# Encoder layer on one core: key and query projections of the second mixer by seven half-size products each

## The chip, the core and the metric

The kernel runs on one core of one Trainium2 chip. The metric is the device time of one execution in microseconds (us); lower is better. TensorE is called PE here, VectorE DVE, ScalarE ACT, GpSimd POOL, and SyncE, which issues DMAs, SP.

## The reference

One layer of a bidirectional encoder, width 1024, sequence 512, batch 1, everything in float32. Cut to what matters:

```python
mod = silu(c) @ w_mod + b_mod                     # nine vectors of 1024: shifts, scales, gates
h = modulate(rmsnorm(x, norm_ffn1), sh1, sc1)
x = x + 0.5 * g1 * swiglu(h, w_ffn1_in, w_ffn1_out)          # first FFN
h = modulate(rmsnorm(x, norm_mix), sh2, sc2)
qa, ka, va, qb, kb, vb, ga, gb = split(h @ w_in)  # 512 128 128 512 512 512 1024 1024 columns
ya = window_gqa_sink(rope(rmsnorm(qa)), rope(rmsnorm(ka)), va, sink) @ w_branch_a
qb = rope(rmsnorm(qb)); kb = rope(rmsnorm(kb))    # per head of 64, 8 heads of each
ob = diff_attention(qb, kb, vb, lam)              # softmax(q1 k1) - lam softmax(q2 k2), times vb
yb = (rmsnorm(ob, subln_b) * (1 - lam_init)) @ w_branch_b
x = x + g2 * ((sigmoid(ga) * ya + sigmoid(gb) * yb) @ w_out)
h = modulate(rmsnorm(x, norm_ffn2), sh3, sc3)
x = x + 0.5 * g3 * swiglu(h, w_ffn2_in, w_ffn2_out)          # second FFN
```

The change concerns `kb` and `qb`, each a product of h (512 x 1024) and a slice of `w_in` (1024 x 512).

## The kernel before, in words

**Products.** Every float32 product is made as three products of shorter floats: an operand is split into a high part (a CAST on ACT) and a low part (original less high, a TENSOR_TENSOR on DVE), both by `split_from` (L190), and high x high, high x low and low x high are added in PSUM. Names: `high` and `low` are the parts of a weight tile, `raw` or `u` its loaded float32, `b` a tile of activations or of their parts, `acc`, `sc`, `op` and `tp` are PSUM banks, `f` and `sm` scratch.

**The FFNs** run their large products as Strassen-Winograd units: a product of 2 x 2 blocks is made of seven products of half size for eight. A `Unit` goes through its items s1, a11, a12, s2, s4, s3, a22; four of these names are sums of blocks of weights (s1 = a21 + a22, s2 = s1 - a11, s3 = a11 - a21, s4 = a12 - s2), made by loading one block with SP and adding another with an accumulating DMA from POOL's queue into the same tile. `MAKE` says how many items ahead a weight is split. The other operand comes from `h_sum` (n1, n2, t3, t4: sums of blocks of h). `two` (L458 to L460) issues a product's instructions, with weights held and 256 columns of h moving.

**The boundary** ends the first FFN, computes the norm, and writes h by `hidden`, in tiles of 128x256: ACT writes the high part (L355), DVE the low part (L363). Three gates are begun beside it, nine PE instructions a tile.

**main** then issues, in this order, the projections of values, keys and queries of the second mixer (`project`, L1202 to L1204: 96 instructions each, h held, 512 columns of weights moving), the remaining gates (`gates`, weights by `load_main`: ACT writes high and the negative, L1132 and L1134, and POOL adds the original by an accumulating DMA, L1135), and the projections of the first mixer (`project_pairs`, L1222 to L1224, h held, 256 columns moving). Of keys and queries each block of 128 rows gets a norm and a rotation: ACT squares (L1255), DVE reduces (L1256), POOL takes the power -1/2 (L1261), DVE multiplies and adds (L1271 to L1274); keys are also multiplied by their norm (L1317), while the query's norm enters later, in the softmax, and `freq` holds its negative (L1340). Then PE transposes (L1281) and the result is split. Scores (L187) follow.

**Order.** Instructions of an engine run in the order in which the program issues them. The pieces of attention are not called where they stand: `Line` keeps an estimate of PE's and DVE's time and calls a piece when it is due (`line.at`, `line.helped`). `beside` puts a column of the modulation product (`mod_col`, a DVE instruction over 128x1024 with its own load of w_mod, L283) after every so many steps of a projection: `LATER` is that number there, `EARLY`, `NEXT` and `SIDE` say how many columns go elsewhere. Tiles come from rings: `raw`, `u` (`u4` in the code), `f` and `b` (`b8`, and `high`, `low`) each have a fixed number of buffers, so a load waits until the last reader of an older tile is done.

Of the kernel before, what the change touches and what calls it, by code (L numbers as in the profile page):

```python
# [11 lines left out]
F32 = mybir.dt.float32  # L12
# [3 lines left out]
ALU = mybir.AluOpType  # L16
AX = mybir.AxisListType

P = 128
# [92 lines left out]

EARLY, NEXT, SIDE, LATER = 3, 3, 0.27, 4
BESIDE_MIX = (1, 2, 2, 2, 2, 1)
# [20 lines left out]
def layer(ctx: ExitStack, tc: tile.TileContext, a: dict):  # L135
# [212 lines left out]
    def hidden(rb, c, sc, sh, hi, lo, r=FULL[0], value=None):  # L348

        t = f2()[:, r]  # L350
        s = modv[sh][:, c : c + 1]
        if value is not None:
            rb = rb[:, r]
        V.scalar_tensor_tensor(t, x[c][:, r], modv[sc][:, c : c + 1], rb, ALU.mult, ALU.mult)
        S.activation(hi[:, r], t, AF.Identity, bias=s)  # L355
        yield
        if value is not None:
            if r.stop - r.start == T:
                t3 = t.rearrange("p (t q) -> p t q", t=2)
            else:  # L360
                t3 = t.unsqueeze(1)
            S.activation(value, t3, AF.Identity, bias=s)
        V.scalar_tensor_tensor(lo[:, r], t, s, f(hi[:, r]), ALU.add, ALU.subtract)  # L363
        yield
# [7 lines left out]
    def boundary(parts, g, norm, sc, sh, hh, hl, into, ahead, at):  # L372
# [16 lines left out]
        def h_steps(rs, r):  # L389

            before = None
# [60 lines left out]
    def two(po, w, k, x, first, last, js=range(2)):  # L452

        (wh, wl), (xh, xl) = w, x
        for j in js:
# [4 lines left out]
            PE.matmul(out, wl[:, s], xh, start=False, stop=last and j == 1, skip_group_check=True)  # L460

    class Unit:

# [13 lines left out]

        in_order, by_columns, asides = (), (), {}
        spare, roomy, apart, more = ("s1",), (), (), {"s1": ("s2", "a11"), "s2": ("s4", "a12"), "a11": ("s3", "a21")}
# [16 lines left out]
        def prepare(self, q):  # L496
# [5 lines left out]
            if q in self.apart:  # L502
                both = b8().rearrange("p a b -> p (a b)")
                hi, lo = both[:, 0:n], both[:, 1024 : 1024 + n]
            else:
                hi, lo = high_low(n, self.asides.get(q, ASIDE), (self, q))
            t = self.at[q]
# [8 lines left out]
        def multiply(self, q, ks=None):  # L516
# [6 lines left out]
            for js in ((0,), (1,)) if q in self.by_columns else (range(2),):  # L523
                for k in ks:
                    x = self.operand(OPERAND[q], k)
                    two(po, self.ready[q], k, x, new and k == 0, k == self.depth - 1, js)
            if self.depth - 1 in ks:
# [20 lines left out]

    def run_items(items):


# [20 lines left out]
        for n, (u, q, ks, also) in enumerate(items):  # L572
            begin(n)
            if also is not None:
                also()
            u.multiply(q, ks)
            if ks is None or u.depth - 1 in ks:
                u.after(q)
            begin(n)
# [21 lines left out]

    def h_sum(t):

        p, q = SUMS[t]
        hq[t] = hq[q if t in ("t3", "t4") else p]

        h_op[t] = [u4() for _ in range(2)] if t == "n1" else b8()
        for i in range(2):
            r = slice(i * T, (i + 1) * T)
            sub(hq[t][:, r], hq[p][:, r], hq[q][:, r], t in NEGATED)  # L610
        for i in range(2):
            v = hq[t][:, i * T : (i + 1) * T].rearrange("p (k q) -> p k q", k=2)
            o = h_op[t][i] if t == "n1" else h_op[t][:, 2 * i : 2 * i + 2, :]
            split_from(o[:, :, T1], o[:, :, T2], v)
# [340 lines left out]
    def item1(u, q, ks=None):  # L955
        items1.append((u, q, ks, side1))

    credit, asked = [0.0], []

    room = b8(F32).rearrange("p a b -> p (a b)")  # L960
    room = [room[:, i * 1024 : (i + 1) * 1024] for i in range(2)]

    def column(columns):
# [5 lines left out]
        if asked and (len(asked) > COLUMNS[columns is rest] or not columns):  # L969
            mod_col(*asked.pop(0), in_order=columns is not later)  # L970

    def side1(n=SIDE):

        while small_loads and len(rest) < 20:
            nc.sync.dma_start(*small_loads.pop())
# [181 lines left out]
    def first_gates(r):  # L1157
# [3 lines left out]
        for k in range(NC):  # L1161
# [7 lines left out]
            yield  # L1169

    vb_w = boundary(
        last1, G1, n2, SC2, SH2, hh, hl, first_gates,
# [17 lines left out]

    def project(srcs, n, then):

        per = 1024 // n
        out = [bank("acc" if t < 3 else "sc") for t in range(NT)]
        for u in range(NC // per):
            wh, wl = srcs.pop(0) if isinstance(srcs, list) else load_halves(srcs[u])
            for t in range(NT):
# [52 lines left out]

    def head_stats(raw, nh, rs, scale8):

        sq = f2()
        n = nh * HD
        S.activation(sq[:, 0:n], raw, AF.Square)  # L1255
        V.tensor_reduce(rs, sq[:, 0:n].rearrange("p (h d) -> p h d", d=HD), axis=AX.X, op=ALU.add)  # L1256
        if scale8:
            V.tensor_scalar(rs, rs, HD * EPS, None, ALU.add)
        else:
            V.tensor_scalar(rs, rs, 1.0 / HD, EPS, ALU.mult, ALU.add)  # L1260
        G.tensor_tensor(rs, rs, half[:, 0:nh], ALU.pow)  # L1261
        return sq

    def rope(raw, nh, tabs, t, z):
        C, R = tabs
        n = nh * HD
        y = f2()
        r3 = raw.rearrange("p (h d) -> p h d", d=HD)
        y3 = y[:, 0:n].rearrange("p (h d) -> p h d", d=HD)
        z3 = z[:, 0:n].rearrange("p (h d) -> p h d", d=HD)  # L1270
        V.tensor_tensor(y3, r3, C[:, t, :].unsqueeze(1).broadcast_to([P, nh, HD]), ALU.mult)  # L1271
        for o, i in ((slice(0, NF), slice(NF, HD)), (slice(NF, HD), slice(0, NF))):
            V.tensor_tensor(z3[:, :, o], r3[:, :, i], R[:, t, o].unsqueeze(1).broadcast_to([P, nh, NF]), ALU.mult)
        V.tensor_tensor(y[:, 0:n], y[:, 0:n], z[:, 0:n], ALU.add)  # L1274
        return y

    def turned(srcs, tag="tp"):
# [10 lines left out]

    def turn_heads(y, nt, t, hi, lo, then=None):
        ht = slice(t * P, (t + 1) * P)  # L1290
        v = turned(cut(y, nt)).rearrange("p (j q) -> p j q", j=nt)
        with tc.high_priority():
            split_from(hi[:, 0:nt, ht], lo[:, 0:nt, ht], v)
        turns["t"] = t + 1
        if then is not None:
            line.at(line.free["tp"] + SLACK, then, SCORES)

    def raws(ps, n=T):
# [5 lines left out]

    def queries(ps, tabs, rq, hi, lo, then):
        for t, raw in enumerate(raws(ps)):
            z = head_stats(raw, 8, rq[:, t, :], True)
            y = rope(raw, 8, tabs, t, z)
            due = line.helped(2.6, 2.5) + SLACK
            line.at(due, lambda y=y, t=t: turn_heads(y, 4, t, hi, lo, then if t == 1 else None), ("tp",))  # L1310

    def keys(raw, nh, tabs, t, hi, lo):
        rs = small(nh)
        z = head_stats(raw, nh, rs, False)
        y = rope(raw, nh, tabs, t, z)
        y3 = y[:, 0 : nh * HD].rearrange("p (h d) -> p h d", d=HD)
        V.tensor_tensor(y3, y3, rs.unsqueeze(2).broadcast_to([P, nh, HD]), ALU.mult)  # L1317
        due = line.helped(0.4 * nh, 2.5) + SLACK
        line.at(due, lambda: turn_heads(y, nh * HD // P, t, hi, lo), ("tp",))
# [6 lines left out]
    done, turns = {"a": 0, "b": 0}, {"a": 0, "b": 0, "o": 0, "w": (0, 0), "q": 0, "t": 0}  # L1326

    def keys_b(ps):
        for t, raw in enumerate(raws(ps)):
            keys(raw, 8, table["kb"], t, kb_h, kb_l)  # L1330

# [4 lines left out]

    def queries_b(ps):
        queries(ps, table["qb"], rqb, qb_h, qb_l, lambda: diff_scores(0, 0))
        for t in range(NT):
            V.tensor_scalar(nrqb[:, t, :], rqb[:, t, :], -1.0, None, ALU.mult)  # L1340

    head_b = {}

    def diff_scores(h, b0):
# [45 lines left out]
        if nxt[0] < 4:  # L1390
            line.at(
                start + 2 * PERIOD_B, lambda: diff_scores(*nxt), SCORES + (lambda: unit - turns["b"] < DEPTH_B - 1 and turns["t"] == NT,)
            )
# [663 lines left out]
def lay_out(i):  # L2057
# [61 lines left out]
```

## Time and profile before

| | |
|---|---|
| median of 3 runs | 1034.4 us (1034.29 to 1034.94) |
| the profiled execution, its own time | 1034.51 us |
| its span in the profile | 1032.7 us |
| busy: PE, DVE, ACT, POOL | 1027.6, 787.4, 582.1, 161.8 us |
| PE instructions (matmul) | 7346 |
| DMA | 220.39 MB, mean 213 GB/s |

The span runs from the first to the last instruction that the profile holds; the execution's time has 1.8 us more around it. The rows of the profile give an engine, the line of the kernel that issued the instruction (L190 is a helper that many call), output and inputs with buffer numbers left out, shapes as partitions x elements, and a count. A row of the timeline begins with its start in us from the start of the span and its duration; in brackets stands how long the engine was idle before it and what ended that. PE overlaps its instructions, so a PE row's duration (0.39) is longer than the step from one start to the next (0.23), and the steps are what counts.

### The profile page before, as it was taken

The page shows a single profiled execution, that of the slowest core. Times are in us where ns is not written, and L with a number is a line of the kernel's source. Part 1 is how long each engine was busy: PE and PEld are TensorE (multiplying, and loading weights), DVE is VectorE, ACT ScalarE, POOL GpSimd, SP SyncE. Part 2 cuts the span into 40 slices and gives each one's busy share as a digit, 9 for nine tenths or more (in the row PEclk, how much of TensorE's full clock was granted, in tenths as well). Part 3 has the DMA queues.
Part 4 walks back from the last instruction along what each step waited for, and adds up shares of the span by engine and source line. Part 5 has one row for each costly group of instructions (what it writes and reads, how often), then busy time and mean ns, then how long its engine had stood idle before and what let it go on. Part 6 is the DMA issues. An engine that isn't in the chain of part 4 may idle for free.

```text
span 1032.7 us, 18848 instructions
## 1 busy us (share of the span) xinstructions
PE 1027.6 (100%) x7346; PEld 949.0 (92%) x7346; DVE 787.4 (76%) x1457; ACT 582.1 (56%) x1013; POOL 161.8 (16%) x189
## 2 busy tenths in 40 slices
PE   9999999999999999999999999999999999999998
PEld 7889899899998998899888888989999999999998
DVE  7886667567787679859772588976898777877877
ACT  6755335244454443668785856525877556655553
POOL 1101110110100100543323101001112112212210
PEclk9999999999999999999999999999999999999999
DMA  9977887967875459796737944974498998989974
GB/s 363 371 207 202 239 241 219 251 153 243 218 188 158 144 213 410 237 281 135 181 79 185 259 136 151 367 250 103 93 239 195 238 236 209 222 228 215 207 158 113
DMA packets 70233, 220.39 MB, mean 213 GB/s; under 512 B 8448, under 2 KB 13184, under 8 KB 70144
## 3 DMA queue, kind: packets, MB, share of 16 engines
q1 hardware_dynamic: 47808, 146.52, 39.2%
q0 software_dynamic: 19200, 68.17, 35.9%
q10 hardware_dynamic: 3136, 4.51, 1.2%
q8 instruction: 57, 0.93, 0.4%
q14 instruction: 32, 0.26, 0.1%
HBM read 208.94 MB, written 10.23 MB: 212 GB/s over the span
## 4 chain that ended last, share of the span: by engine, by line
PE 96%; DVE 2%; ACT 2%; issue 0%; POOL 0%; DVEq 0%; ACTq 0%
PE acc L460 7%; PE acc L459 7%; PE acc L458 7%; PE sc L460 6%; PE sc L458 6%; PE sc L459 6%; PE sc L174 5%; PE sc L176 5%; PE sc L175 5%; PE acc L174 5%; PE acc L176 5%; PE acc L175 5%; PE tp L1281 2%; PE acc L709 2%; PE acc L1203 2%; PE acc L1202 2%
## 5 line engine op out<-in xcount | busy, mean ns | idle before, releaser
L190 ACT CAST high<-raw 128x1024 fp32r<-128x1024 f32 (+2 forms) x176 | 158.4, 914 | 149.4 <-PE sc L175 40.8
L190 DVE TENSOR_TENSOR low<-raw,high 128x1024 fp32r<-128x1024 f32 (+2 forms) x176 | 183.5, 1052 | 40.4 <-ACT high L190 38.8
L459 PE MATMUL acc<-b,high 128*128 128x256 f32 x508 | 140.5, 277 | 0.1
L458 PE MATMUL acc<-b,high 128*128 128x256 f32 x508 | 140.6, 277 | 0.0
L460 PE MATMUL acc<-b,low 128*128 128x256 f32 x508 | 140.5, 277 | 0.0
L460 PE MATMUL sc<-b,low 128*128 128x256 f32 x500 | 138.0, 276 | 0.0
L458 PE MATMUL sc<-b,high 128*128 128x256 f32 x500 | 138.0, 276 | 0.0
L459 PE MATMUL sc<-b,high 128*128 128x256 f32 x500 | 138.0, 276 | 0.0
L190 ACT CAST high<-u 128x1024 fp32r<-128x1024 f32 (+1 forms) x73 | 75.4, 1034 | 52.3 <-PE sc L175 20.0
L190 DVE TENSOR_TENSOR low<-u,high 128x1024 fp32r<-128x1024 f32 (+1 forms) x73 | 87.7, 1201 | 21.5 <-ACT high L190 20.0
L174 PE MATMUL sc<-b,high 128*128 128x512 f32 (+1 forms) x272 | 97.4, 358 | 0.0
L175 PE MATMUL sc<-b,high 128*128 128x512 f32 (+1 forms) x272 | 97.0, 357 | 0.0
L176 PE MATMUL sc<-b,low 128*128 128x512 f32 (+1 forms) x272 | 97.0, 357 | 0.0
L459 PEld LDWEIGHTS acc<-b,high 128*128 128x128 f32 x508 | 95.4, 188 | 0.5 <-DVE b L1903 0.3
L458 PEld LDWEIGHTS acc<-b,high 128*128 128x128 f32 x508 | 95.4, 188 | 0.2
L460 PEld LDWEIGHTS acc<-b,low 128*128 128x128 f32 x508 | 95.4, 188 | 0.1
L460 PEld LDWEIGHTS sc<-b,low 128*128 128x128 f32 x500 | 93.9, 188 | 0.0
L458 PEld LDWEIGHTS sc<-b,high 128*128 128x128 f32 x500 | 93.9, 188 | 0.0
L459 PEld LDWEIGHTS sc<-b,high 128*128 128x128 f32 x500 | 93.9, 188 | 0.0
L174 PE MATMUL acc<-b,high 128*128 128x512 f32 (+1 forms) x240 | 89.2, 372 | 0.0
L176 PE MATMUL acc<-b,low 128*128 128x512 f32 (+1 forms) x240 | 86.6, 361 | 0.0
L175 PE MATMUL acc<-b,high 128*128 128x512 f32 (+1 forms) x240 | 86.5, 360 | 0.0
(400 smaller groups left out, 2717.9 us busy)
## 6 DMA issues: line engine op xcount, KB each, us to landing
u<-w_mod SPq DMA_DIRECT2D x38, 512.0 KB, 8.0
b<-w_mod SPq DMA_DIRECT2D x32, 512.0 KB, 5.5
raw<-w2i SPq DMA_DIRECT2D x31, 512.0 KB, 5.6
u<-w2i POOLq DMA_DIRECT2D x31, 512.0 KB, 6.8
raw<-w1u SPq DMA_DIRECT2D x24, 512.0 KB, 6.5
u<-w1u POOLq DMA_DIRECT2D x24, 512.0 KB, 7.1
raw<-w1o SPq DMA_DIRECT2D x24, 384.0 KB, 4.8
raw<-w_gate SPq DMA_DIRECT2D x16, 512.0 KB, 5.4
```

Of the source, the lines that this page charges most:

```text
L174: PE.matmul(out, wh, xh, start=first, stop=False)
L175: PE.matmul(out, wh, xl, start=False, stop=False)
L176: PE.matmul(out, wl, xh, start=False, stop=last)
L190: last = S.copy(hi, src), V.tensor_tensor(lo, src, f(hi), ALU.subtract)
L458: PE.matmul(out, wh[:, s], xh, start=first and j == 0, stop=False, skip_group_check=True)
L459: PE.matmul(out, wh[:, s], xl, start=False, stop=False, skip_group_check=True)
L460: PE.matmul(out, wl[:, s], xh, start=False, stop=last and j == 1, skip_group_check=True)
L709: PE.matmul(out1[i][:, r], w[:, i * P : (i + 1) * P], h[:, r], start=first and r.start == 0, stop=last and r.stop == T, skip_group_check=True,
L1202: PE.matmul(out[t][:, 0:n], hh[k][:, ht], wh[:, o : o + n], start=k == 0, stop=False)
L1203: PE.matmul(out[t][:, 0:n], hh[k][:, ht], wl[:, o : o + n], start=False, stop=False)
L1281: PE.transpose(tp[:, j * P : (j + 1) * P], src, ident)
```

## The change

Keys and queries are each made by a `Unit`: seven products of half size, with h held and 256 columns of weights moving (`two_turned`), 7 x 24 = 168 instructions where 96 of 512 columns stood. The weights are laid out by quarters. The first sum of weights (s1) of the key's unit is loaded and added ahead of the boundary. `hidden` writes h also as float32 (an ACT instruction for each tile, L356), from which the four sums of h are made at the start of `main`. Results come by quarters of 256 rows and 256 columns (two blocks of rows, four heads), in the unit's order, and the norm and rotation are made by `two_blocks`, which the first mixer had already: L1507 ACT square, L1508 reduce, L1513 POOL's power, L1515 to L1520 rotation, L1333 the key's norm, L1350 the query's negated norm. Scores may be issued when all four key quarters and the first query quarter are turned. Columns: eight more go beside the first FFN (which gives up a `u` buffer to their loads), fewer beside the projections (every 10th step of the values, every 12th of the units, every 2nd of the gates). In this part SP issues in the program's order.

The core of the diff:

```diff
-EARLY, NEXT, SIDE, LATER = 3, 3, 0.27, 4
+EARLY, NEXT, SIDE, LATER = 4, 2, (0.27, 0.55), (10, 12, 2)
...
-            S.activation(value, t3, AF.Identity, bias=s)
+            S.activation(value, t, AF.Identity, bias=s)
...
             for c in range(NC):
-                h = hidden(rs, c, sc, sh, hh[c], hl[c], r)
+                value = hq[f"b{c // 4 + 1}{n}"][:, c % 4 * H : (c % 4 + 1) * H]
+                h = hidden(rs, c, sc, sh, hh[c], hl[c], r, value)
...
+    def two_turned(po, w, k, x, first, last, js=range(2)):
+
+        (wh, wl), (xh, xl) = w, x
+        s = slice(k * 2 * P, (k + 1) * 2 * P)
+        for j in js:
+            r = slice(j * P, (j + 1) * P)
+            out = po[:, j * H : (j + 1) * H]
+            PE.matmul(out, xh[:, r], wh[:, s], start=first and j == 0, stop=False, skip_group_check=True)
+            PE.matmul(out, xl[:, r], wh[:, s], start=False, stop=False, skip_group_check=True)
+            PE.matmul(out, xh[:, r], wl[:, s], start=False, stop=last and j == 1, skip_group_check=True)
...
-    room = [room[:, i * 1024 : (i + 1) * 1024] for i in range(2)]
+    room = [room[:, i * 1024 : (i + 1) * 1024] for i in range(2)] + [u4(F32).rearrange("p a b -> p (a b)")]
...
-        while small_loads and len(rest) < 20:
+        while small_loads and len(rest) < 28:
...
+    def projected(w, post, odd):
+        u = Unit([w[i] for i in range(4)], 4, h1_operand, post, odd)
+        u.srcs = dict(zip(("a11", "a12", "a21", "a22"), u.srcs))
+        u.products, u.aside = two_turned, -ASIDE
+        u.in_order = ("s1", "s2", "s3", "s4", "a22")
+        return u
+
+    key_unit, query_unit = projected(a["w_kb"], lambda *by: keys_b(*by), 1), projected(a["w_qb"], lambda *by: queries_b(*by), 0)
...
+    key_unit.ask("s1")
     vb_w = boundary(
...
+    def queries_b(c, v, u):
+        n, i, raw = quarter(c, v)
+        rs = rqb[:, 2 * i : 2 * i + 2, 4 * n : 4 * n + 4]
+        y = two_blocks(raw, 4, table["qb"], i, rs, True)
+        V.tensor_scalar(nrqb[:, 2 * i : 2 * i + 2, 4 * n : 4 * n + 4], rs, -1.0, None, ALU.mult)
...
+            if (n, i) == (0, 0):
+                line.at(
+                    line.free["tp"] + SLACK, lambda: diff_scores(0, 0), SCORES + (lambda: len(keys_done) == 4,)
+                )
...
-        yield from beside(project(vb_w, T, values_b), LATER)
-        yield from beside(project(a["w_kb"], T, keys_b), LATER)
-        yield from beside(project(a["w_qb"], T, queries_b), LATER)
-        yield from beside(gates(lambda: gate_next[0] < EARLY_A), 1)
+        with tc.manual_schedule(engines={mybir.EngineType.SP}):
+            k, q = key_unit, query_unit
+            with tc.issue_after(split[0]), tc.issue_after(split[1]):
+                k.prepare("s1")
+            h_sum("n1", False)
+            for t in ("n2", "t3", "t4"):
+                h_sum(t, False)
...
+            yield from beside(project(vb_w, T, values_b, also), LATER[0])
+            items = [(k, p, None, None) for p in ("s1", "a11", "a12", "s2", "s4", "s3")]
+            items += [(q, "s1", None, None), (k, "a22", None, None)]
+            items += [(q, p, None, None) for p in ("a11", "a12", "s2", "s4", "s3", "a22")]
+            yield from beside(item_steps(items, MM3), LATER[1])
+            yield from beside(gates(lambda: gate_next[0] < EARLY_A), LATER[2])
...
-    for nm, m in (("w_kb", kb), ("w_qb", qb), ("w_vb", vb)):
-        o[nm] = con(m.reshape(4, 2, P, 512).transpose(0, 2, 1, 3)).reshape(4, P, 1024)
+    o["w_vb"] = con(vb.reshape(4, 2, P, 512).transpose(0, 2, 1, 3)).reshape(4, P, 1024)
+    for nm, m in (("w_kb", kb), ("w_qb", qb)):
+        o[nm] = con(m.reshape(2, 4, P, 2, 256).transpose(3, 0, 2, 1, 4)).reshape(4, P, 1024)
```

DVE where the first block of queries gets its norm and rotation, before (numbers after a name tell tiles apart; `raw_3213` are the tables of the rotation, `f_399` and `f_400` the block's scratch, `mod_101` the columns' sums):

```order
L283 ISA u_394_4221,mod_101<-u_394_4221,ka_96,par 128x1024
L283 ISA mod_101 128x1
L190 TENSOR_TENSOR b_325_3707<-tp_4205,b_324_3706 128x4x128
L1271 TENSOR_TENSOR f_400_4237<-f_395_4224,raw_3213 128x512
L1256 TENSOR_REDUCE rqb<-f_399_4232 128x8
L1258 TENSOR_SCALAR rqb<-rqb 128x8
L1273 TENSOR_TENSOR f_399_4232<-f_395_4224,raw_3213 128x8x32 x2
L1340 TENSOR_SCALAR freq_3713<-rqb 128x8
L1274 TENSOR_TENSOR f_400_4237<-f_400_4237,f_399_4232 128x512
```

The same place in the changed kernel (`f_385` and `f_386` are the quarter's scratch, `raw_3924` and `raw_4150` weights of the query's unit, `tp_4319` the last key quarter turned, `tp_4386` the first query quarter):

```order
L1515 TENSOR_TENSOR f_386_4293<-f_382_4255,raw_3231 128x512
L1508 TENSOR_REDUCE rqb<-f_385_4292 128x2x4
L190 TENSOR_TENSOR low<-raw_3924,high 128x1024
L190 TENSOR_TENSOR b_329_3746<-tp_4319,b_328_3745 128x2x2x128
L1510 TENSOR_SCALAR rqb<-rqb 128x2x4
L1517 TENSOR_TENSOR f_385_4292<-f_382_4255,raw_3231 128x8x32 x2
L1350 TENSOR_SCALAR freq_3752<-rqb 128x2x4
L190 TENSOR_TENSOR low<-raw_4150,high 128x1024
L1520 TENSOR_TENSOR f_386_4293<-f_386_4293,f_385_4292 128x512
L555 TENSOR_TENSOR f_388_4338<-f_388_4338,acc_4152 128x512
```

Between the negated norm (`freq`) and the add that ends the rotation (L1520) there is now a weight's low part, and weight and turning work stands among the rotation's instructions.

POOL from the first key norm on, before (`sm` are norms of keys, `rqb` of queries):

```order
L1261 TENSOR_TENSOR sm_4024<-sm_4024,half 128x8
L1261 TENSOR_TENSOR sm_4036<-sm_4036,half 128x8
L1135 DMA low<-w_gate 128x1024
L1261 TENSOR_TENSOR sm_4048<-sm_4048,half 128x8
L1135 DMA low<-w_gate 128x1024
L1135 DMA low<-w_kva 128x1024 x2
L1261 TENSOR_TENSOR rqb<-rqb,half 128x8
```

And in the changed kernel:

```order
L522 DMA u_350_3916<-w_qb 128x1024
L1513 TENSOR_TENSOR sm_4084<-sm_4084,half 128x8
L1513 TENSOR_TENSOR sm_4135<-sm_4135,half 128x8
L1513 TENSOR_TENSOR sm_4214<-sm_4214,half 128x8
L1513 TENSOR_TENSOR rqb<-rqb,half 128x2x4
L1156 DMA low<-w_gate 128x1024 x2
L1156 DMA low<-w_kva 128x1024
L1513 TENSOR_TENSOR rqb<-rqb,half 128x2x4
L1156 DMA low<-w_kva 128x1024
```

The first gates' accumulating loads stand behind the power of the first query quarter instead of among those of the keys, and the second quarter's power stands between the two loads of w_kva.

More of the change, by code (lines that the diff above doesn't have):

```diff
@@ L525, in multiply @@
                     x = self.operand(OPERAND[q], k)
-                    two(po, self.ready[q], k, x, new and k == 0, k == self.depth - 1, js)
+                    self.products(po, self.ready[q], k, x, new and k == 0, k == self.depth - 1, js)
             if self.depth - 1 in ks:
@@ L549, in run_items, with item_steps @@
     def run_items(items):
+        for _ in item_steps(items):
+            pass
+    def item_steps(items, cost=None):
         due, at, now = [], [], 0.0
@@ L575, in run_items @@
                 also()
-            u.multiply(q, ks)
+            if cost is None:
+                u.multiply(q, ks)
+                yield
+            else:
+                for k in range(u.depth):
+                    u.multiply(q, [k])
+                    yield cost
             if ks is None or u.depth - 1 in ks:
@@ L600, in h_operand, with h_sum @@
         return t[:, k, T1], t[:, k, T2]
-    def h_sum(t):
+    def h_sum(t, spare=True):
         p, q = SUMS[t]
         hq[t] = hq[q if t in ("t3", "t4") else p]
-        h_op[t] = [u4() for _ in range(2)] if t == "n1" else b8()
+        spare = spare and t == "n1"
+        h_op[t] = [u4() for _ in range(2)] if spare else b8()
         for i in range(2):
@@ L1287, in cut @@
         return [src[:, j * P : (j + 1) * P] for j in range(n)]
[L1289 to L1296, printed above, removed]
     def raws(ps, n=T):
@@ L1325, in layer, with quarter, turn_quarter, keys_b @@
     ob_h, ob_l = b8(), b8()
[L1326 to L1330, printed above, removed]
+    done, turns = {"a": 0, "b": 0}, {"a": 0, "b": 0, "o": 0, "w": (0, 0), "q": 0}
+    keys_done, queries_done = set(), set()
+    def quarter(c, v):
+        if c == "c21":
+            v = raws([v])[0]
+        return int(c[1]) - 1, int(c[2]) - 1, v.rearrange("p (t h d) -> p t h d", t=2, d=HD)
+    def turn_quarter(y, n, i, hi, lo):
+        v = turned(cut(y, 4)).rearrange("p (t j q) -> p t j q", t=2, j=2)
+        with tc.high_priority():
+            split_from(
+                *(
+                    t[:, 2 * n : 2 * n + 2, 2 * i * P : 2 * (i + 1) * P].rearrange("p j (t q) -> p t j q", t=2)
+                    for t in (hi, lo)
+                ),
+                v,
+            )
+    def keys_b(c, v, u):
+        n, i, raw = quarter(c, v)
+        rs = small(8)
+        y = two_blocks(raw, 4, table["kb"], i, rs.rearrange("p (t h) -> p t h", t=2), False)
+        y3 = y.rearrange("p (h d) -> p h d", d=HD)
+        V.tensor_tensor(y3, y3, rs.unsqueeze(2).broadcast_to([P, 8, HD]), ALU.mult)
+        def turn():
+            turn_quarter(y, n, i, kb_h, kb_l)
+            keys_done.add((n, i))
+        line.at(line.helped(3.2, 2.5) + SLACK, turn, ("tp",))
     def values_b(ps):
@@ L1335, in values_b, with turn @@
             line.helped(0.6)
[L1337 to L1340, printed above, removed]
+    def queries_b(c, v, u):
+        n, i, raw = quarter(c, v)
+        rs = rqb[:, 2 * i : 2 * i + 2, 4 * n : 4 * n + 4]
+        y = two_blocks(raw, 4, table["qb"], i, rs, True)
+        V.tensor_scalar(nrqb[:, 2 * i : 2 * i + 2, 4 * n : 4 * n + 4], rs, -1.0, None, ALU.mult)
+        def turn():
+            turn_quarter(y, n, i, qb_h, qb_l)
+            queries_done.add((n, i))
+            if (n, i) == (0, 0):
+                line.at(
+                    line.free["tp"] + SLACK, lambda: diff_scores(0, 0), SCORES + (lambda: len(keys_done) == 4,)
+                )
+        line.at(line.helped(2.6, 2.5) + SLACK, turn, ("tp",))
     head_b = {}
@@ L1391, in diff_scores @@
             line.at(
-                start + 2 * PERIOD_B, lambda: diff_scores(*nxt), SCORES + (lambda: unit - turns["b"] < DEPTH_B - 1 and turns["t"] == NT,)
+                start + 2 * PERIOD_B, lambda: diff_scores(*nxt), SCORES + (lambda: unit - turns["b"] < DEPTH_B - 1 and (nxt[0] // 2, nxt[1] // 2) in queries_done,)
             )
```

76 lines of the change are left out of this document (23 added, 53 removed).

## The prediction

> **What bounds the kernel now.** I read the engines' busy shares first, then the chain that ended last, then PE's waits, then the same shares by stage.
>
> ```profile
> PE 1027.6 (100%) x7346; PEld 949.0 (92%) x7346; DVE 787.4 (76%) x1457; ACT 582.1 (56%) x1013; POOL 161.8 (16%) x189
> ...
> PE 96%; DVE 2%; ACT 2%; issue 0%; POOL 0%; DVEq 0%; ACTq 0%
> ```
>
> ```profile
> PE acc L634 <- DVE sm L640: 0.9, 1, 0.9
> PE acc L187 <- DVE u L190: 0.2, 1, 0.2
> ```
>
> PE is busy throughout, is 96% of the chain, and waits 1.1 us in all. So a product less is worth its full time, if what feeds PE keeps up. Whether it can is a matter of stages (stretch, then busy us of PE, weight loads, DVE, ACT, POOL, each with its count; granted clock, DMA share, GB/s):
>
> ```profile
> 300.00:340.00 40.00, 39.95 (x279) 36.90 (x278) 29.67 (x52) 19.73 (x27) 2.41 (x6) 1.00 0.60 179
> 340.00:374.00 34.00, 34.00 (x288) 33.83 (x287) 25.93 (x56) 17.45 (x33) 4.13 (x7) 1.00 0.25 81
> 374.00:396.00 22.00, 22.00 (x99) 18.20 (x98) 16.75 (x29) 4.97 (x10) 0.00 (x0) 1.00 1.01 389
> 396.00:440.00 44.00, 44.00 (x200) 36.40 (x199) 39.77 (x79) 23.48 (x44) 13.19 (x8) 1.00 0.84 304
> ```
>
> The rows are the end of the first FFN, the boundary, the value projection, and the key and query projections. In the last DVE works 39.77 of 44.00 us: it is nearly a second bound there. The granted clock is 1.00 throughout. The profiled run took 1034.51 us round a span of 1032.7, and the median is 1034.4; I sum on the profiled run and take off 0.1 at the end.
>
> **The change part by part.** *The products.* PE's rows at the borders of the key and query projections, at one half-size product of the FFN, and where the kernel already holds h and moves 256 columns of weights:
>
> ```profile
> 309.17 0.28 PE L458 MATMUL acc<-b,high 128*128 128x256 f32 x1
> ...
> 311.89 0.28 PE L458 MATMUL acc<-b,high 128*128 128x256 f32 x1
> ```
>
> ```profile
> 395.39 0.39 PE L1202 MATMUL acc<-high,b 128*128 128x512 f32 x1
> 417.15 0.39 PE L1202 MATMUL acc<-high,b 128*128 128x512 f32 x1
> 439.90 0.39 PE L174 MATMUL acc<-b,high 128*128 128x512 f32 x1
> 451.27 0.28 PE L1222 MATMUL acc<-high,b 128*128 128x256 f32 x1
> ...
> 454.08 0.28 PE L1222 MATMUL acc<-high,b 128*128 128x256 f32 x1
> ...
> 466.43 0.74 PE L187 MATMUL sc<-b,b 64*128 64x512 f32 x3
> 468.03 0.39 PE L1222 MATMUL acc<-high,b 128*128 128x256 f32 x1
> ...
> 470.65 0.28 PE L1222 MATMUL acc<-high,b 128*128 128x256 f32 x1
> ...
> 473.03 0.28 PE L1222 MATMUL acc<-high,b 128*128 128x256 f32 x1
> ```
>
> The key projection is 96 instructions of 512 columns in 417.15 − 395.39 = 21.76 us (0.2267 each). The query projection takes 22.75; the 0.99 more are two groups of four transposes, 0.5 each. Removed: 2 × 21.76 = 43.5 us. Added: 2 units × 7 products × 24 = 336 instructions of 256 columns. In the FFN 24 of them take 2.72 us (0.1133); with h stationary 24 take 2.81 (0.117) from 451.27, but 21 take 2.38 (0.1133) from 470.65. I take 0.1133, the later and the FFN's figure: 38.1 us; at 0.117 it would be 39.3. PE's gain is 5.4, or 4.2 at the least. The transposes stay eight groups of four.
>
> [...]
>
> *Work at the boundary.* 16 more ACT activations write h as f32, one for each of eight 128x256 tiles of both halves of the rows. ACT's rows there, and then DVE's low part of the first tile and the PE instruction that first uses it:
>
> ```profile
> 354.36 0.51 ACT L355 ACTIVATE b<-f,mod 128x256 fp32r<-128x256 f32 x1 [0.28 <-DVE f L354]
> 355.14 0.51 ACT L355 ACTIVATE b<-f,mod 128x256 fp32r<-128x256 f32 x1 [0.28 <-DVE f L354]
> ```
>
> ```profile
> 352.66 0.48 DVE L363 SCALAR_TENSOR_TENSOR b<-f,mod,b 128x256 fp32r<-128x256 f32 x1 [0.19 <-ACT b L355]
> ...
> 354.77 0.28 PE L174 MATMUL acc<-b,u 128*128 128x256 f32 x1
> ```
>
> ACT comes round every 0.78 us, as DVE's two instructions a tile let it, with 0.51 of work; a second one of that length makes its round up to 1.02. PE needs about as long for a tile: three gates of three instructions, 9 × 0.117 = 1.05, so ACT keeps its lead. The first low part is done at 353.14 and PE takes it at 354.77, so 1.6 us cover the start. I price it at 0; without that cover a tile would cost up to 1.02 − 0.78 = 0.24, eight of them 1.9, and no gain is possible.
>
> *Sums of h and columns.* Four sums of h are 8 DVE subtractions and their splits, beside the value projection. DVE there has 8 subtractions and 8 lows at 0.60, four or five weight lows at 1.15 and three columns at 1.21 (durations below), 9.6 + 5.2 + 3.6 = 18 us, where 16.75 stood in 374:396 before, in 22. The key's product s1 wants the first sum and its own low part, which stand early in that row, at 395.4. The cover is the 96 instructions of the values; gone, each sum would cost its 2.4 us once. Price 0, up to 1. Eight columns go to the FFN: 8 × 1.21 us of DVE, where 10 of 40 us are free, and 8 × 0.5 MB of loads, where the DMA engines are 0.60 busy. A third buffer for them takes one from the FFN's s1 weights:
>
> ```profile
> raw<-w1u SPq DMA_DIRECT2D x24, 512.0 KB, 6.5
> u<-w1u POOLq DMA_DIRECT2D x24, 512.0 KB, 7.1
> ```
>
> Load and accumulation take 13.6 us; s1 is made five products ahead (5 × 2.72 = 13.6), so two buffers still turn over inside a unit of 7 × 2.72 = 19 us each. What hides a late s1 is that lead of 13.6; if it is gone, a unit holds PE up to one product, 2.7. Price 0 to 2.7; I take 0, since the row of 300:340 shows PE whole at 39.95 of 40.
>
> *DVE between the first key sum and the first scores.* This carries the forecast. Durations, start to start:
>
> ```profile
> 429.02 0.16 DVE L1260 TENSOR_SCALAR sm<-sm 128x8 f32<-128x8 f32 x1
> 429.09 0.68 DVE L1271 TENSOR_TENSOR f<-f,raw 128x512 f32<-128x512 f32 x1
> 429.69 0.75 DVE L1273 TENSOR_TENSOR f<-f,raw 128x256 f32<-128x256 f32 x2
> 430.36 0.69 DVE L190 TENSOR_TENSOR low<-raw,high 128x512 fp32r<-128x512 f32 x1
> ...
> 434.41 1.28 DVE L283 CUSTOM_DVE_ANT_0 u<-u,ka,par 128x1024 f32<-128x1024 f32 x1
> 435.62 0.08 DVE L283 DVE_READ_ACCUMULATOR2_ANT mod<- 128x1 f32 x1
> ...
> 368.47 4.63 DVE L190 TENSOR_TENSOR low<-raw,high 128x1024 fp32r<-128x1024 f32 x4 [0.45 <-ACT high L190]
> ```
>
> A 512-wide sum, multiply or reduction is 0.60, a small one 0.07, a pair of half rotations 0.67, a weight's low part about 1.15 (4.63 / 4), a column 1.21. PE ends key product a12 72 instructions after 395.4, at 403.6; weight lows ahead of the first key sum put its start at about 404.8 (estimate; 403.6 at best). From it to the first query quarter's half rotations the order has 26 of 0.60, five pairs, six weight lows, five small ones: 15.6 + 3.4 + 6.9 + 0.4 = 26.3, so 431. Then DVE's next instruction negates the query's norm, which POOL's power makes:
>
> ```profile
> 444.36 0.17 DVE L1340 TENSOR_SCALAR freq<-rqb 128x8 f32<-128x8 f32 x1 [1.22 <-POOL rqb L1261]
> ...
> 428.94 0.95 POOL L1135 DMA_DIRECT2D low<-w_gate  x1 [2.02 <-ACT low L1134]
> 429.60 4.17 POOL L1261 TENSOR_TENSOR sm<-sm,half 128x8 f32<-128x8 f32 x1
> ...
> 442.38 0.76 DVE L1273 TENSOR_TENSOR f<-f,raw 128x256 f32<-128x256 f32 x2
> ...
> 442.56 1.77 POOL L1261 TENSOR_TENSOR rqb<-rqb,half 128x8 f32<-128x8 f32 x1 [5.85 <-PE acc L175]
> ```
>
> DVE lost 1.22 us there before; now the same wait stands ahead of a weight low (1.15) and the add (0.60) that the query's transposes need. So they can start at about 431 + 1.3 + 1.8 = 434.1. PE is there after 305 products and four groups of transposes: 395.4 + 34.6 + 2.0 = 432.0. Stall: 2.1. Behind it the scores' last four need the transposes' low part, which DVE makes after an add, a column and a multiply (about 0.6 us late), and the product a22 needs a bank that DVE empties next (0.6). Together 3.3; if the first key sum starts at its best time, 2.1.
>
> *Gate 1 next.* Its low part is an accumulating load behind that same power on POOL, which ends at about 432.3:
>
> ```profile
> raw<-w_gate SPq DMA_DIRECT2D x8, 512.0 KB, 9.2
> ...
> low<-w_gate POOLq DMA_DIRECT2D x3, 512.0 KB, 8.5
> raw<-w_kva SPq DMA_DIRECT2D x2, 512.0 KB, 4.4
> ```
>
> It lands at 440.8, or 439.4 at the FFN's 7.1. PE, unstalled, comes at 432.0 + 0.5 + 0.8 (seven products) + 1.6 (scores, 466.43 to 468.03) + 2.7 = 437.6. That is 1.8 to 3.2 late, in parallel with the stalls above: the larger counts, not the sum. Were DVE quicker, this load would be late next. I take 3.0 for both.
>
> Sum: 1034.5 − 43.5 + 38.1 + 3.0 = 1032.1, and 1032.0 on the median's footing.
>
> **The rivals.** *All hidden.* The 26 us of DVE start at once at 403.6, the power lasts less than the half rotations and gate 1's low part comes in 5 us as its raw neighbour does: 1034.4 − 5.4 = 1029.0. For it: 24 columns of 1.21 stood in this stage before and seven or so stand there now (17 × 1.21 = 20 us of DVE and 17 × 0.5 = 8.5 MB less). Against it: two separate chains arrive late by the same 2 to 3 us.
>
> *POOL's queue, ending slower.* The powers of the second to fourth query quarters now stand behind accumulations of gate and kva weights, which wait for ACT, which waits for a raw load, which SP issues in program order behind column loads. The negation holds all of DVE meanwhile. If the kva load (issued at about 425.5, an estimate: in the count above that is when the query's s4 has its low part and leaves a buffer to a column that loads ahead of it) lands in the gates' 9.2 us rather than its own 4.4, ACT ends its low part at about 437.5 and the power at 440.5; each of three quarters then holds PE some 1.5 to 2 us. 3 × 1.8 = 5.4 on top of 3.0 gives 1037.4. It turns slower once the kva load takes over about 8 us. For it: POOL's 4.17 and the 2.02 us wait for ACT above; against: fewer columns load at that time. [...]
>
> *Slower products.* At 0.117 throughout, with the same stalls: 1033.2.
>
> *The FFN starved of a buffer.* One s1 late by a product adds 2.7 to the forecast: 1034.7. Against it: the lead above.
>
> **How the numbers follow.** A measurement tells about 0.2%, 2.1 us, from no change: faster is below 1032.3, slower above 1036.5. Forecast (stalls of 2 to 4 us: 1031.0 to 1033.0) 0.42, of which two thirds are faster; all hidden 0.24; POOL's queue 0.18, two thirds of it slower; slower products 0.10 and a starved FFN 0.06, nearly all within. That the change doesn't do what it says has no share: the counts of its instructions are fixed. Faster 0.28 + 0.24 = 0.52, slower 0.12 and 0.02 for the rest, same 0.34. The range leaves out the best tenth of the hidden case and the worst of POOL's: 1028.9 to 1037.0.
>
> **What would show it.** Right: 336 products of 256 columns at 0.113, ending in a wait of PE on DVE at the first query transposes (1.5 to 3 us), small ones at L187 and on the bank, gate 1 within 1 us of its low part, no wait at 340:374. Wrong: PE waits of 1 us or more in the FFN or at the boundary; waits at all query quarters; or none at all, and a span 5.4 shorter.

## The result, and the profile after

The changed kernel takes 1080.7 us (median of 4 runs, 1080.2 to 1083.1) against 1034.5 before (median of 4): a ratio of 1.0451, 95% interval 1.0433 to 1.0469. It is slower by 46 us where I forecast 2.4 us faster, in a range of 1028.9 to 1037.0. The profiled execution took 1080.23 us around a span of 1078.5.

The busy shares and the chain, of the changed kernel:

```profile
PE 1039.7 (96%) x7490; PEld 964.0 (89%) x7490; DVE 807.1 (75%) x1477; ACT 596.2 (55%) x1035; POOL 168.1 (16%) x197
...
PE 23%; issue 2%; DMA 2%; ACT 0%; POOL 0%; DVE 0%; DVEq 0%; POOLq 0%; ACTq 0%
```

PE was idle for 5 us of the span before (1032.7 less 1027.6); now it is idle for 39 us (1078.5 less 1039.7). Waits and idle time of PE are counted here as the profile counts them, from the end of one instruction to the start of the next. Its longest waits (us in total, times, longest us):

```profile
PE sc L456 <- ACT f L545: 16.7, 7, 4.2
PE tp L1288 <- DVE u L190: 8.8, 1, 8.8
PE acc L174 <- ACT high L190: 1.7, 1, 1.7
PE tp L1288 <- DVE f L1520: 1.5, 1, 1.5
```

By stage (stretch, then busy us of PE, weight loads, DVE, ACT, POOL; granted clock, DMA share, GB/s):

```profile
20.00:150.00 130.00, 130.00 (x735) 113.68 (x734) 100.00 (x143) 67.01 (x96) 10.57 (x12) 1.00 0.75 234
150.00:350.00 200.00, 181.41 (x1266) 170.09 (x1265) 132.38 (x192) 77.78 (x104) 20.04 (x23) 0.96 0.75 215
350.00:380.00 30.00, 28.91 (x183) 25.95 (x182) 21.63 (x43) 11.33 (x18) 4.41 (x7) 1.00 0.66 215
380.00:470.00 90.00, 87.01 (x641) 81.50 (x639) 79.57 (x144) 59.15 (x102) 20.98 (x19) 1.00 0.68 199
470.00:520.00 50.00, 40.95 (x278) 36.50 (x279) 40.35 (x105) 29.32 (x63) 13.62 (x12) 0.90 0.90 263
```

PE idles 18.6 us in the first FFN (150 to 350), where the diff moves nothing but columns and a buffer. It idles 3.0 in the stretch of the values, keys and queries, and 9.0 just behind. In both bad stretches the granted clock is below 1 (0.96, 0.90).

The borders of the products on PE:

```profile
425.63 0.28 PE L467 MATMUL sc<-high,b 128*128 128x256 f32 x1
...
473.15 0.39 PE L174 MATMUL acc<-b,high 128*128 128x512 f32 x1
```

The key's product began at 395.39 and begins at 425.63: 30.2 us are lost before the first half-size product. Gate 1 began at 439.90 and begins at 473.15, 33.25 late. The 3.0 in between come from work that changed places: first scores and three groups of transposes, about 3.3 us, now stand ahead of the gate and stood behind it before. So the products and their stalls together neither gained nor lost. The rest, 12 us and some small waits, is lost after gate 1.

**The first FFN.** SP's load of an s1 weight, ahead of the first of the waits, in the kernel before and then in the changed one:

```profile
131.44 0.38 SPq L492 DMA_DIRECT2D u<-w1u  x1
```

```profile
146.94 0.33 SPq L501 DMA_DIRECT2D u<-w1u  x1
...
145.69 1.22 DVE L190 TENSOR_TENSOR low<-u,high 128x1024 fp32r<-128x1024 f32 x1 [0.20 <-ACT high L190]
...
151.19 0.88 POOL L503 DMA_DIRECT2D u<-w1u  x1 [22.09 <-DMA u<-w1u]
...
160.77 1.04 ACT L190 CAST high<-u 128x1024 fp32r<-128x1024 f32 x1 [7.26 <-DMA u<-w1u]
...
162.24 0.58 ACT L545 COPY f<-sc 128x512 f32<-128x512 f32 x1
...
162.87 0.38 PE L456 MATMUL sc<-b,high 128*128 128x256 f32 x1 [3.29 <-ACT f L545]
```

The load is issued 15.5 us later. It goes out 0.03 us after DVE has made the low part of the weight that held the buffer (145.69 + 1.22 = 146.91). POOL adds the second block once the first has landed, 151.19, and that lands near 160.8. ACT stands at the cast for 7.26 us; behind it in ACT's order is the copy that empties a PSUM bank, and PE waits for the bank. The buffer had been held for 40 us or more, since no load of an s1 weight went out between 106.58 and this one. At the two other places where PE waits, the load (225.11 and 294.70) also goes out within 0.03 us of the end of a low part.

### The profile page after: what moved, and what is told of

It is laid out like the page before. It is cut to its first block, busy times and chain, and to the rows that moved or that the text cites. A ratio compares the mean times of both kernels' runs of the same rounds, so it can differ in the third digit from the quotient of the medians.

```text
span 1078.5 us, 19169 instructions
## 1 busy us (share of the span) xinstructions
PE 1039.7 (96%) x7490; PEld 964.0 (89%) x7490; DVE 807.1 (75%) x1477; ACT 596.2 (55%) x1035; POOL 168.1 (16%) x197
## 5 line engine op out<-in xcount | busy, mean ns | idle before, releaser
L456 PE MATMUL sc<-b,high 128*128 128x256 f32 x500 | 142.8, 286 | 16.7 <-ACT f L545 16.7
L458 PE MATMUL sc<-b,low 128*128 128x256 f32 x500 | 141.7, 283 | 0.2 <-DVE low L190 0.2
L457 PE MATMUL sc<-b,high 128*128 128x256 f32 x500 | 141.8, 284 | 0.0
L456 PE MATMUL acc<-b,high 128*128 128x256 f32 x508 | 140.9, 277 | 0.9 <-DVE f L547 0.9
L190 DVE TENSOR_TENSOR low<-u,high 128x1024 fp32r<-128x1024 f32 (+1 forms) x76 | 91.3, 1202 | 45.4 <-ACT high L190 44.1
L190 ACT CAST high<-u 128x1024 fp32r<-128x1024 f32 (+1 forms) x76 | 78.6, 1034 | 76.5 <-DMA u<-w1u 21.3
L456 PEld LDWEIGHTS sc<-b,high 128*128 128x128 f32 x500 | 97.5, 195 | 18.1 <-ACT f L545 18.1
L458 PEld LDWEIGHTS sc<-b,low 128*128 128x128 f32 x500 | 97.5, 195 | 0.4 <-DVE low L190 0.4
L457 PEld LDWEIGHTS sc<-b,high 128*128 128x128 f32 x500 | 97.7, 195 | 0.0
L456 PEld LDWEIGHTS acc<-b,high 128*128 128x128 f32 x508 | 95.5, 188 | 1.4 <-DVE f L547 1.3
```

What stands on the lines that cost most here:

```text
L190: last = S.copy(hi, src), V.tensor_tensor(lo, src, f(hi), ALU.subtract)
L456: PE.matmul(out, wh[:, s], xh, start=first and j == 0, stop=False, skip_group_check=True)
L457: PE.matmul(out, wh[:, s], xl, start=False, stop=False, skip_group_check=True)
```

## The experiments

"Two buffers" is the changed kernel with two loading buffers for the FFN's columns in place of three:

```diff
-    room = [room[:, i * 1024 : (i + 1) * 1024] for i in range(2)] + [u4(F32).rearrange("p a b -> p (a b)")]
+    room = [room[:, i * 1024 : (i + 1) * 1024] for i in range(2)]
```

**Which part of the change costs the FFN its 28 us.** Theory 1 blames the buffer, theory 2 the columns. First the two buffers:

> The changed kernel with two loading buffers for the FFN's columns as before, so the FFN's s1 weights keep all their u buffers; its eight extra columns stay. Theory 1 (the buffer taken from s1 delays its load, ACT waits for it in order and PE for ACT): the three groups of waits in the first FFN go, some 25 us, and the time is about 1054. Theory 2 (the eight extra columns themselves, by DVE time and loads, slow the FFN): the waits stay and the time is within 3 us of 1080.7.

Measured: 1052.95 us, ratio to before 1.0164 (1.0120 to 1.0208), so 27.8 less than the changed kernel. The seven waits of L456 on ACT are one of 0.5 us. Next the line above put the other way into the kernel before, alone:

> The kernel before with the third loading buffer taken from the u ring, and nothing else of the change: no column more in the FFN. Theory 1: the FFN waits appear here too, 20 to 28 us, time 1055 to 1062. Theory 2: nothing happens, 1034 to 1036.

Measured: 1067.66 us, ratio 1.0306 (1.0245 to 1.0367): 32.5 us slower by one buffer, above the 1055 to 1062 that I wrote. The edit also gives the columns a third loading buffer; that it is the buffer taken which costs, and not the one given, I read from the rows above, where the load waits for its buffer. PE's row of that kernel:

```profile
PE sc L458 <- ACT f L536: 20.9, 7, 6.1
```

Then the columns without the buffer, in the kernel before:

```diff
-EARLY, NEXT, SIDE, LATER = 3, 3, 0.27, 4
+EARLY, NEXT, SIDE, LATER = 4, 2, (0.27, 0.55), 4
...
-        while small_loads and len(rest) < 20:
+        while small_loads and len(rest) < 28:
```

> The kernel before with eight more columns beside the first FFN and eight fewer beside the projections, with its two loading buffers. Theory 1: no wait of PE in the FFN, 1033 to 1036. Theory 2: 20 us or more in the FFN, above 1054.

Measured: 1036.86 us, ratio 1.0019 (1.0005 to 1.0034). PE is idle for 0.7 us between 150 and 350. So eight columns cost the FFN next to nothing; the buffer costs nearly all of it. Theory 1 holds from both sides.

**The wait behind gate 1.** Theory 3: columns beside the gates hold DVE. In the expectations I call what PE waits for there the first mixer's keys. PE's rows show something else, the transposes of the second mixer's attention weights (`x`): the next group of them needs the PSUM bank `tp`, which DVE empties with a low part. In the two-buffer kernel:

```profile
472.43 0.60 PE L1288 MATMUL tp<-ident,x 128*128 128x128 f32 x4
...
483.66 0.69 PE L1288 MATMUL tp<-ident,x 128*128 128x128 f32 x2 [8.58 <-DVE u L190]
```

I first spread the columns (`LATER` (5, 8, 2)), on two buffers:

> As the first of these, with the sixteen later columns spread over values (every 5th step) and units (every 8th), so that none stands in a block between the gates and the first mixer's keys. Theory 3 (the block of eight columns, each waiting for a load that stands late in SP's program order, holds DVE ahead of the key split that PE's transposes need: 8.8 us of wait and a slow clock behind it): 10 to 12 us less than the first of these, about 1043. Rival (DVE is short in the units: moving columns there costs what it saves): within 3 us of the first.

Measured: 1057.82 us (1.0211, 1.0167 to 1.0255), 5 slower than two buffers alone. The wait of 8.6 us is gone, but PE is idle for 11.6 us between 380 and 470, where it was 3.7. Neither side foresaw a loss: DVE works 79 of these 90 us, and the columns cost as much there. So I moved them out of the stretch, eight of them and then all sixteen, into the FFN, on two buffers. For the eight, with a faster pace there (`SIDE`):

```diff
-EARLY, NEXT, SIDE, LATER = 4, 2, (0.27, 0.55), (10, 12, 2)
+EARLY, NEXT, SIDE, LATER = 5, 1, (0.42, 0.75), (10, 14, 2)
...
-        while small_loads and len(rest) < 28:
+        while small_loads and len(rest) < 36:
```

> The changed kernel with two loading buffers, and eight of the sixteen later columns moved on into the first FFN, at a faster pace there (SIDE 0.42, 0.75), so that eight stay behind and at most three stand in a block ahead of the first mixer's keys. Theory 3 (a block of columns whose loads come late holds DVE ahead of the key split, 8.6 us of PE's wait and 1.7 of slow clock in the kernel with two buffers at 1053): the wait falls below 2 us, and the faster pace frees the gate weights' loads (3 us of wait at the boundary): about 1040 to 1043. Rival (DVE is short in the whole stretch, the wait only moves, as it did when the columns were spread): 1050 or more.

Measured: 1050.33 us (1.0154, 1.0124 to 1.0183). The wait is gone, as theory 3 says, but the time is that of the rival: with sixteen columns more than before PE is idle for 5.3 us in the FFN (150 to 350), and for 5.0 between 380 and 520.

> All sixteen later columns in the first FFN (SIDE 0.55, 0.85), none beside the projections. If DVE's columns are all that keeps the half-size products from paying, PE waits less than 1 us between 380 and 480 and the time is 1029 to 1032, if the FFN bears 24 columns more. If the chains of the products themselves (power, weight lows, bank copies) are late, as forecast, 3 to 4.5 us of waits stay there: 1032 to 1036. If the FFN does not bear the columns, waits show before 350 us.

> The kernel before with the same placing of columns as the last one, products unchanged: the control. If the FFN bears the columns: 1033 to 1036. The difference of the two is what the half-size products are worth with the columns out of their way: minus 5 if nothing stalls, minus 1 to minus 2 if the forecast's stalls stand.

Measured: 1057.94 us (1.0227, 1.0197 to 1.0257) and, for the control, 1052.76 (1.0177, 1.0144 to 1.0210). The FFN does not bear 24 columns more: between 20 and 350 PE is idle for 11.5 and, in the control, 9.7 us. With no column beside the products 2.5 us of idle time stay between 380 and 470, where the control has none: those belong to the products' own chains. The seven products' kernel comes out 5 us slower than the control, where I expected it faster by 1 to 5. The profiled executions, 6.9 apart, show where: 4.3 lie ahead of the key's first product (415.32 against 410.99), in the FFN and at the boundary, 0.8 between it and gate 1, and 1.7 behind. So this pair says little about the products.

The block of columns by itself: two buffers, with the last of the later columns left out (their sums hold only the bias). I wrote eight; the trace has 7 loads of these columns where the two-buffer kernel has 16, so nine are left out, the eight of the block and one beside the gates.

> The kernel with two loading buffers (1053), without the last eight of the later columns: their products with w_mod and their loads are left out, only the bias is copied. Theory 3 (these eight columns, beside the two gates, hold DVE 18 us, 8 of them for loads that SP issues late, ahead of the key split that PE's transposes need): the wait of 8.6 us at the first mixer's key transposes and the slow clock behind it go, 1042 to 1044. Rival (the key chain is late by its own weights' loads, columns only fill the time): the wait stays above 5 us, 1049 or more.

This and the next three ran on a chip where the kernel before spread from 1034.4 to 1036.9, and two executions of one kernel lay up to 6.6 apart, so I read their waits and not their totals. The profiled execution took 1044.91 us (median 1047.64 of two, ratio 1.0114, 1.0045 to 1.0183), a little above the 1042 to 1044 that I wrote. The wait of 8.6 us is gone: the second group of these transposes starts at 465.04 with no idle time. A wait of 1.6 stands ahead of the first group. Theory 3 holds, in that the columns hold DVE ahead of what PE waits for. What held DVE there, in the two-buffer kernel (SP, then DVE, then PE's clock in 2 us stretches):

```profile
451.78 4.07 SPq L1149 DMA_DIRECT2D raw<-w_gate  x3
461.90 2.46 SPq L245 DMA_DIRECT2D u<-w_mod  x2
464.47 1.44 SPq L1149 DMA_DIRECT2D raw<-w_gate  x1
466.63 1.53 SPq L245 DMA_DIRECT2D u<-w_mod  x2
...
473.04 1.28 DVE L283 CUSTOM_DVE_ANT_0 u<-u,ka,par 128x1024 f32<-128x1024 f32 x1 [2.81 <-DMA u<-w_mod]
476.55 1.28 DVE L283 CUSTOM_DVE_ANT_0 u<-u,ka,par 128x1024 f32<-128x1024 f32 x1 [2.21 <-DMA u<-w_mod]
479.82 1.28 DVE L283 CUSTOM_DVE_ANT_0 u<-u,ka,par 128x1024 f32<-128x1024 f32 x1 [1.99 <-DMA u<-w_mod]
...
482.93 0.68 DVE L190 TENSOR_TENSOR u<-tp,u 128x512 fp32r<-128x512 f32 x1
```

```profile
484.00:486.00 2.00, 2.00 (x10) 1.47 (x10) 2.00 (x8) 1.11 (x2) 1.58 (x2) 0.50 0.04 8
486.00:488.00 2.00, 2.00 (x10) 1.16 (x9) 1.61 (x6) 0.00 (x0) 1.48 (x2) 0.50 0.36 94
488.00:490.00 2.00, 2.00 (x16) 2.00 (x16) 2.00 (x6) 1.36 (x3) 0.00 (x0) 0.80 1.02 248
```

DVE waits 7 us for three of the columns' loads, in order, and the low part at 482.93, for which PE has waited since 475, stands behind. I expected the loads to be late by their place in SP's order, between loads of gate weights. The trace shows less of that: SP issues each of these four within 0.02 us of the column that frees its buffer (461.88, 464.02, 466.62, 467.82), and they land 11.1 to 13.2 us later, while the DMA engines are busy throughout (share 1.03 from 440 to 480). So the columns wait for each other and for full DMA engines. Behind the wait PE runs four us at half clock.

**The power ahead of the query's transposes**, on two buffers: the negation of the norm (`V.tensor_scalar(nrqb...)`) moved into `turn`, behind `turn_quarter`.

> The kernel with two loading buffers, with the negation of the query's norm issued behind the query's transposes, so that DVE does not stand at POOL's power ahead of the rotation's last add. If that wait (1.5 us on DVE) is what makes the first query transposes late, PE's wait of 1.5 us there goes and the time falls by 1 to 2 us, to about 1051.5. If DVE is late by its own load, the wait moves by less than 0.5 us and the time stays at 1053.

Measured on that chip: 1061.15 us (1.0244, 1.0195 to 1.0293). With two buffers alone, and here:

```profile
435.95 2.08 POOL L1513 TENSOR_TENSOR rqb<-rqb,half 128x8 f32<-128x8 f32 x1 [7.41 <-DVE rqb L1510]
437.99 1.81 POOL L1156 DMA_DIRECT2D low<-w_gate  x2
...
438.07 0.17 DVE L1350 TENSOR_SCALAR freq<-rqb 128x8 f32<-128x8 f32 x1 [1.53 <-POOL rqb L1513]
```

```profile
441.64 3.81 POOL L1513 TENSOR_TENSOR rqb<-rqb,half 128x8 f32<-128x8 f32 x1 [7.44 <-DVE rqb L1510]
445.41 1.81 POOL L1156 DMA_DIRECT2D low<-w_gate  x2
...
454.13 0.80 PE L176 MATMUL acc<-b,low 128*128 128x512 f32 x1 [5.29 <-DMA low<-w_gate]
```

DVE no longer waits ahead of the rotation's add (it waits 0.93 us behind it), PE's wait at the first query transposes is gone, and gate 1's low part is late by 5.29 us. That is what the prediction named as late next; it is worse than the 1.8 to 3.2 there. The power takes 3.81 us where it took 2.08, and the load lands 8.7 us after it. The time, forecast at about 1051.5, did not fall.

**The rate of the products.** They step at 0.118 us; `u.aside` 32 columns further on:

> The kernel with two loading buffers, with the units' weights 32 columns further on in their tiles (the offset that the FFN's units have). The half-size products ran at 0.118 us where the forecast took 0.1133. If the place of the operands in memory sets that, most of the fourteen products run at 0.1133 and the time falls by 1 to 1.5 us. If holding h and moving weights is what costs it, or the load on memory from other engines, the steps stay at 0.117 to 0.118.

Measured: 1062.65 us (1.0259, 1.0218 to 1.0299). The second of the key's products, 24 steps, in the two-buffer kernel and here:

```profile
401.66 0.28 PE L467 MATMUL sc<-high,b 128*128 128x256 f32 x1
...
404.49 0.28 PE L467 MATMUL op<-high,b 128*128 128x256 f32 x1
```

```profile
405.66 0.28 PE L467 MATMUL sc<-high,b 128*128 128x256 f32 x1
...
408.38 0.28 PE L467 MATMUL op<-high,b 128*128 128x256 f32 x1
```

2.83 us against 2.72. Six of the fourteen now run at 0.113 to 0.114, against two before, but eight stay at 0.117 to 0.118, and the time did not fall. That the place in memory does it is not shown: with the place unchanged the count of fast products differs from run to run as well, two to four in most and nine in the run with the columns spread. Moving weights past a held h is not the cause by itself, since products of that kind run at both rates; what sets the rate is open.

**The boundary.** Two buffers, columns in the FFN at a faster pace (`SIDE` (0.34, 0.62)):

> The kernel with two loading buffers, with the FFN's columns at a faster pace (SIDE 0.34, 0.62), so that the last ones load before the last weights of the FFN. If late column loads on SP's queue are what delays those weights and the first gates' (3.5 us of waits of PE at 343 to 350 us), the waits there fall below 1 us and the time by 2 to 3, to about 1050.5. If the extra f32 copy of h or the key's first sum of weights is what costs it, they stay.

Measured: 1057.73 us (1.0211, 1.0130 to 1.0292). The waits at 343 to 350, 2.8 us of idle time with two buffers, are down to 0.3, with the f32 copy of h and the key's first sum still in place. So it was the late columns that delayed the last weights of the FFN and the first gates'. But 3.4 us of idle time appear between 249 and 300, and nothing is won.

No run points to a version that beats the kernel before: the best that makes every column, at 1050, still carries some 10 us of idle time in the FFN and the mixer's stretch, against less than 4 us of gain.

## Why the prediction was wrong

*The sums of h and columns: this step failed.* I wrote that a third loading buffer takes one from s1 and "two buffers still turn over inside a unit of 7 x 2.72 = 19 us each. Price 0 to 2.7; I take 0". It measured 27.8 us when given back and 32.5 when taken from the kernel before. Two errors lie in it. The sum counted the load and the accumulation, 13.6, and not the time that the buffer is held after them, through s2 and s4, which use the same tile: 40 us at least, by the rows of the first FFN. And I took the row of 300:340, PE whole, for a margin: it shows that the supply sufficed with all buffers, and says nothing of how close it was. The price of a late s1 was not "one product, 2.7": in the changed kernel pairs of waits (3.29 and 1.83, 4.15 and 2.55, 2.44 and 1.78) stand at three places, with a slow clock behind all of them but that of 1.83, because the late cast holds ACT and with it the copies that empty PE's banks.

*Columns beside the gates: a term left out.* I counted the columns that leave the units as relief ("17 x 1.21 = 20 us of DVE less") and never priced where they go. Eight of them land in a block on DVE, with loads that come late, ahead of a low part of the attention weights that empties PE's bank: 8.6 to 8.8 us of wait and a granted clock of 0.50 behind it.

*The products: right in kind, mis-sized.* I took 0.1133 a step, 38.1 us, with 39.3 at 0.117. Without the waits among them the 336 steps took 40.0 us, 0.119 on average, and 40.1 in the two-buffer kernel; the 192 before, counted the same way, took 43.8. The gain is 3.7 to 3.8, below the 4.2 that I called the least.

*DVE and POOL at the first query quarter: right in kind, and partly by luck in size.* The wait on the power was forecast at 1.3 and is 1.53. PE's wait at these transposes was forecast at 2.1 and is 1.5; the scores' low part 0.6, measured 0.3; the bank 0.6, measured 0.5. All idle time from the key's first product to gate 1 is 3.3 us in the changed kernel and 3.7 with two buffers, where I took 3.0; but the three forecast waits make only 2.3 of it, and 0.8 is a wait for a bank inside the key's unit that I had not foreseen. Gate 1 stood behind it as the next thing late. What made the late power take 3.81 us is open. DVE's work beside it does not explain it by itself: in the changed kernel a power of the same shape took 1.77 us at 438.35, with DVE at work throughout, and the one at 462.10, beside a waiting DVE, took 2.08.

*The boundary: the extra copy of h at 0 was right*, as the run with the faster pace shows; the 2.8 us that appear there with two buffers come from the columns.

*The rivals.* "POOL's queue" did not happen: in the changed kernel the transposes of the second to fourth query quarters (474.53, 480.79, 487.46) start with no idle time of PE. "The FFN starved of a buffer" did, with a chance of 0.06 and a price ten times too small.

## What to carry to other kernels

A buffer taken from a ring is a change to the schedule of everything that the ring feeds: price it by how long one tile is held, from its load to its last reader (40 us at least here), over the number of buffers left, and not by whether the bound engine was whole before. Work that a change pushes away has to be followed to where it lands, with its loads and the buffers that these wait for. And a late operand costs whoever waits for anything behind it in its engine's order: here a weight's cast, for which ACT stood 7.26 us, held the copies that free PE's banks, and PE waited 3.29.

## What the hardware showed that I had not expected

PE's granted clock fell to 0.50 behind five of the six longest waits in the first FFN of the changed kernel, so that these stalls cost more than their length. Behind the wait of 3.29 us that ended at 162.87:

```profile
162.00:164.00 2.00, 1.13 (x7) 1.14 (x8) 1.67 (x2) 0.81 (x2) 0.57 (x1) 0.87 1.09 285
164.00:166.00 2.00, 2.00 (x12) 2.00 (x11) 0.39 (x1) 1.04 (x1) 0.30 (x1) 0.50 1.03 268
166.00:168.00 2.00, 2.00 (x15) 2.00 (x15) 2.00 (x3) 0.53 (x2) 0.00 (x0) 0.77 1.05 280
```

By these rows the granted clock is 0.50 for about 3.4 us (0.5, 2.0 and 0.9), and the 256-column step is 0.213 there instead of 0.113, some 1.6 us more. It does not follow length alone: a wait of 1.83 us at 172 left the clock at 1.00, one of 1.78 at 319.7 brought it to 0.52 (the mean of 322 to 324). Behind the waits of 2.44, 2.55 and 4.15 us it was 0.57, 0.56 and 0.50 in the 2 us stretches from 310, 252 and 242. What decides whether it falls is not shown. Ahead of the key's first product PE issues the same 2570 instructions in both kernels; of the 30.2 us lost there 19.6 are more idle time and 10.6 are slower work. Five such stretches of half clock make about 8 of these, an estimate from 1.6 each.
